# The end of a MoE router: rows of expert 0 by products of split parts, and a new order around them

## The chip, the cores and the metric

The kernel runs on one core of a Trainium2 chip. The metric is the device time of one execution in microseconds, given as the median of several runs. Beside these runs one execution was taken by the hardware profiler; all rows below come from it. TensorE multiplies, VectorE, ScalarE and GpSimd work on elements, SP issues DMAs; each works through a queue of its own in order.

## The reference

One decoder layer on 512 tokens of width 1024, in fp32: two token mixers, merged, then a mixture of experts, then an embedding gate. What matters here is the mixture of experts:

```
def hier_moe(h, w_rg, b_rg, w_re, b_re, w_e13, w_e2):
    t = h.reshape(b * s, dm)
    gl = (t @ w_rg) + b_rg                      # 4 groups
    pg = softmax(gl); gsel = top-1 of gl
    el = ((t @ w_re) + b_re)                    # 4 groups x 4 experts
    elg = el of the chosen group
    ev, ei = top_k(elg, 2)
    wts = pg[gsel] * softmax(ev)
    gate[token, expert] = wts
    a = t @ w_e13[e]                            # 1024 -> 2 x 256, 16 experts
    act = silu(g_) * u * gate
    y = sum over e of act @ w_e2[e]             # 256 -> 1024
```

Here h is the rms-normalized x after x = x + mixed @ w_out. The chip's products of full accuracy are made by splitting an fp32 value into a high part (fp32r) and a low part (the rest), and adding three products: high by high, high by low, low by high.

## The kernel before

**Weights.** All weights come as pieces of 128 x 1024 fp32 (512 KB) through one `Stream`. `_load` issues the DMA of a piece into a ring of raw buffers (WE, WE2, WR and WE3, 28 pieces for the experts' weights). `_split` makes the high part on ScalarE (L103) and the low part on VectorE (L106) into one of 4 slots of the pool WS; with `late_low` set, the low part is kept back as a function to be called later (L97 to L101). `ahead` and `get` run loads and splits in front of the use, `split_ahead` pieces, within `limit` and `raw_limit`. WE3's buffers are tiles of the pool `mx` (`freed`), which first hold mT, the split parts of the mixed output; so a load into them (tile name mT) waits until a block's products with mT are done.

**Router.** Tokens are worked on in four blocks b of 128. x2 holds x after the output product, half by half (c = 0, 1 of 512 columns). For each block the loop L1304 multiplies the second half (L1315, 24 products), adds it to x2 on VectorE (L1323), and calls `half`: GpSimd scales x2 into t (L1239), a DMA writes t to t_dram (L1240; ScalarE's queue for c = 0, SP's for c = 1), TensorE transposes x2 into tp (L1243), tp is copied to tT, and ScalarE squares for the norm (L1247). `logits` multiplies tT by the router's weights (L1255). `choose` (L1266 to L1285) is a chain of small VectorE instructions: norm, logits, best group, two best experts, hot, and then products on TensorE that count the tokens' places (pos_ps). `route` (L1288) makes oh0, the one-hot of a token's place within expert 0 (L1294), posk and two one-hots more, and multiplies these into slot_ps (L1300). choose and route of block b run inside block b + 1; those of the last block stand behind the loop.

**Router's end, L1327 to L1376.** `rows0` (L1332) gathers the rows of expert 0 on TensorE: acc0 += oh0 x t, in fp32, for four blocks and two halves. Two loads go to GpSimd's queue, three high parts of expert 0's weights to ScalarE (L97). After choose and route of the last block acc0 is copied to r0, one half by ScalarE and one by VectorE (L1362), gidx is made (L1363), the first low part lows[0] is made, r0 is transposed (L1369) and split into t0 (L1370, L1371), and rsl and the low parts that are left follow. cnt (L1359) is the largest count of an expert; all engines load it and branch over a block for overfull experts (L1413).

**Experts.** `gather(e)` fetches the rows of expert e from t_dram into tg by an indirect DMA from GpSimd (L1378), three experts ahead. The exponentials for the tokens' weights wts follow (L1384 to L1398); wts is first used behind the experts (L1651). `expert_in(e)` makes 24 products of 512 columns (L1510); `expert_T(e)` transposes tg and splits it into tgh and tgl (L1496 to L1498); for expert 0, `between` calls `expert_T(1)` ahead of the last of its four weight pieces (MID = 3). `expert_act` (silu, L1408), `expert_actT` and `expert_out` (L1535, 12 products; ye copied on ScalarE, L1539, and scattered to y_dram by GpSimd, L1540) follow. Behind the experts come `pp_start` and `pp_mm` (L1574), the loads of yy from y_dram, and the last stage.

**What sets the order.** The instructions are traced in the order of the text; a scheduler then orders each engine's queue by its own clock, an instruction that is ready early going ahead of an earlier traced one that is not. `issue_after(i)` (and `after`) ties what a block traces on i's engine behind i; `in_order()` ties all that it traces on each engine into the order of the text.

## Time and profile before

| | |
|---|---|
| time, median of 3 runs | 705.02 us (704.5 to 706.92) |
| the profiled execution | 707.7 us, of which the span from first to last instruction is 705.9 us |
| TensorE / VectorE / ScalarE / GpSimd busy | 684.4 (97%) / 561.5 (80%) / 434.5 (62%) / 139.1 us (20%) |
| granted TensorE clock | 0.998 of full speed |
| HBM | 108.41 MB read, 12.58 MB written, 171 GB/s over the span |

How to read it: busy times are those in which an engine ran an instruction; register, branch, semaphore and DMA-issuing instructions do not count. The router's loop runs from about 437 to 470 us, its end to 482, the sixteen experts to about 636, the last stage to 706. Matmuls overlap, so the distance between two starts is the cost of one, not its duration. A gap in a timeline stands in brackets with what ended it.

### The profile page before, as it was taken

To read this page: it belongs to the slowest core of one execution; us is meant where nothing else is said; L and a number is where in the kernel's file an instruction comes from. 1 tells how busy PE (TensorE), PEld (TensorE's weight loads), DVE (VectorE), ACT (ScalarE), POOL (GpSimd) and SP (SyncE) were. 2 spreads that over 40 slices of the span, in tenths; PEclk is the share of its full clock that TensorE was granted. 3 is DMA by queue.
4 is the path that set the end of the run, shared out by engine and by line. 5 is a ranking of instruction groups with operands and counts; after the bars stand their busy time and mean duration, and the time that the engine had idled before them with its cause. 6 is when DMAs were issued, how large, how long until landed. Compare 5 with 4: busy or idle time off the path is not lost.

```text
span 705.9 us, 11369 instructions
## 1 busy us (share of the span) xinstructions
PE 684.4 (97%) x3813; PEld 579.5 (82%) x3813; DVE 561.5 (80%) x1430; ACT 434.5 (62%) x848; POOL 139.1 (20%) x189
## 2 busy tenths in 40 slices
PE   8999989999999999999999999999999999999995
PEld 5889967789999998888888888876788888887784
DVE  5768988888768668878775763768999999986986
ACT  5547756576556765665453242236999999987642
POOL 5510033234334210000000002122222222110000
PEclk9999999999999999999999999999999999999999
DMA  8435631222212113232229348945999989507511
GB/s 290 110 96 151 168 100 37 84 61 61 61 31 59 32 40 82 61 91 64 86 63 354 121 124 284 372 150 189 384 386 374 370 299 364 234 30 265 194 61 61
DMA packets 81992, 113.72 MB, mean 161 GB/s; under 512 B 9417, under 2 KB 49945, under 8 KB 81930
## 3 DMA queue, kind: packets, MB, share of 16 engines
q1 hardware_dynamic: 72322, 97.14, 41.5%
q0 software_dynamic: 5648, 11.53, 4.5%
q10 hardware_dynamic: 3960, 4.29, 1.8%
q8 instruction: 31, 0.51, 0.3%
q14 instruction: 31, 0.25, 0.1%
HBM read 108.41 MB, written 12.58 MB: 171 GB/s over the span
## 4 chain that ended last, share of the span: by engine, by line
PE 74%; DVE 8%; DMA 7%; ACT 4%; issue 4%; POOL 3%; ACTq 0%; SPq 0%; POOLq 0%; DVEq 0%
PE S L1510 12%; PE mm L979 12%; PE mm L292 7%; PE mm L1682 6%; PE mm L1535 6%; PE mm L1151 6%; PE mm L802 3%; PE mm L1315 3%; PE tp L896 2%; DMA wr<-in_w_re 2%; PE S L875 2%; PE tp L1496 2%; DVE wlWS L106 2%; PE mm L912 1%; ACT whWS L103 1%
## 5 line engine op out<-in xcount | busy, mean ns | idle before, releaser
L106 DVE TENSOR_TENSOR wlWS<-rawWR,whWS 128x1024 fp32r<-128x1024 f32 (+3 forms) x75 | 85.9, 1153 | 25.5 <-ACT whWS L103 24.6
L103 ACT ACTIVATE whWS<-rawWR 128x1024 fp32r<-128x1024 f32 (+1 forms) x76 | 79.1, 1049 | 35.7 <-PE tp L1223 7.0
L106 DVE TENSOR_TENSOR wlWS<-rawWE,whWS 128x1024 fp32r<-128x1024 f32 x58 | 69.2, 1222 | 3.6 <-ACT whWS L103 2.3
L103 ACT ACTIVATE whWS<-rawWE 128x1024 fp32r<-128x1024 f32 x58 | 60.6, 1071 | 5.1 <-PE S L1510 4.1
L292 PE MATMUL mm<-wlWS,hTh 128*128 128x256 f32 (+1 forms) x184 | 54.2, 295 | 0.1
L292 PE MATMUL mm<-whWS,hTl 128*128 128x256 f32 (+1 forms) x184 | 54.2, 294 | 0.0
L292 PE MATMUL mm<-whWS,hTh 128*128 128x256 f32 (+1 forms) x184 | 53.9, 293 | 0.0
L979 PE MATMUL mm<-hTh,whWS 128*128 128x512 f32 x128 | 50.3, 393 | 0.0
L886 POOL TENSOR_SCALAR pr<-pr,sm 128x128 f32<-128x128 f32 (+3 forms) x64 | 34.7, 554 | 78.7 <-DVE sm L884 34.8
L979 PE MATMUL mm<-hTh,wlWS 128*128 128x512 f32 x128 | 50.0, 391 | 0.0
L979 PE MATMUL mm<-hTl,whWS 128*128 128x512 f32 x128 | 50.0, 391 | 0.0
L1510 PE MATMUL S<-whWS,tgh 128*128 128x512 f32 x120 | 48.6, 405 | 0.0
L1510 PE MATMUL S<-wlWS,tgh 128*128 128x512 f32 x120 | 47.8, 398 | 0.0
L1510 PE MATMUL S<-whWS,tgl 128*128 128x512 f32 x120 | 47.3, 395 | 0.0
L880 ACT ACTIVATE pr<-pr,sm 128x128 f32<-128x128 f32 (+3 forms) x64 | 35.4, 555 | 17.0 <-DVE sm L878 16.8
L899 ACT ACTIVATE ph<-tp 128x512 fp32r<-128x512 f32 (+1 forms) x48 | 25.1, 522 | 20.3 <-PE tp L896 19.8
L108 POOL TENSOR_TENSOR wlWS<-rawWR,whWS 128x384 fp32r<-128x384 f32 (+1 forms) x17 | 25.2, 1484 | 62.0 <-ACT whWS L103 57.1
L292 PEld LDWEIGHTS mm<-wlWS,hTh 128*128 128x128 f32 x184 | 34.9, 190 | 0.4 <-DVE wlWS L106 0.3
L292 PEld LDWEIGHTS mm<-whWS,hTl 128*128 128x128 f32 x184 | 34.9, 190 | 0.1
L292 PEld LDWEIGHTS mm<-whWS,hTh 128*128 128x128 f32 x184 | 34.9, 190 | 0.0
L1540 POOL DMA_INDIRECT y_dram<-ye,gidx x16 | 20.8, 1302 | 62.1 <-ACT aeh L1524 59.0
L876 DVE CUSTOM_DVE_ANT_0 pr<-S,strip 128x128 f32<-128x128 f32 (+3 forms) x64 | 29.3, 485 | 3.9 <-PE S L875 3.4
(492 smaller groups left out, 2076.8 us busy)
## 6 DMA issues: line engine op xcount, KB each, us to landing
rawWE<-in_w_e SPq DMA_DIRECT2D x59, 512.0 KB, 9.1
rawWR<-in_w_in SPq DMA_DIRECT2D x40, 512.0 KB, 3.9
mT<-in_w_e SPq DMA_DIRECT2D x22, 512.0 KB, 10.5
rawWR<-in_w_e SPq DMA_DIRECT2D x13, 512.0 KB, 10.1
rawWR<-in_w_out SPq DMA_DIRECT2D x8, 512.0 KB, 4.0
yy<-y_dram SPq DMA_DIRECT2D x8, 512.0 KB, 5.1
rawWR<-in_w_ck SPq DMA_DIRECT2D x4, 512.0 KB, 4.4
rawWR<-in_w_cv SPq DMA_DIRECT2D x4, 512.0 KB, 5.6
```

The source lines that it names most:

```text
L103: self.last_hi = self.nc.scalar.activation(h[:, :n], flat, AF.Copy)
L106: self.last = self.nc.vector.tensor_tensor(l[:, :c], flat[:, :c], h[:, :c].bitcast(F32), OP.subtract)
L108: self.nc.gpsimd.tensor_tensor(l[:, c:n], flat[:, c:], h[:, c:n].bitcast(F32), OP.subtract)
L292: T.matmul(dst[b], a[:, kk, b * P:(b + 1) * P], w[:, kk - k0, :n], start=(kk == 0 and i == 0 and b % share == 0), stop=(kk == NK - 1 and i ...
L876: V.tensor_tensor_reduce(pr[:, hh, :n], s_[:, :n], strip[:, 512 - q0:640], 0.125, -3.0e38, OP.add, OP.max, sm[:, 0, hh:hh + 1])
L880: A.activation(pr[:, hh, :n], pr[:, hh, :n], AF.Exp, bias=sm[:, 1, hh:hh + 1], accum_out=sm[:, 2, hh:hh + 1])
L886: G.tensor_scalar(pr[:, hh, :n], pr[:, hh, :n], sm[:, 3, hh:hh + 1], 1.0, op0=OP.mult, op1=OP.mult)
L979: T.matmul(ps, w[:, k], a[:, k], start=(k == 0 and i == 0), stop=(k == NK - 1 and i == 2))
L1151: T.matmul(ps, w[:, k, f * P:(f + 1) * P], a[:, k], start=(k == 0 and i == 0), stop=(k == 3 and i == 2))
L1510: T.matmul(ps, a[:, 2 * m + k], w[:, k], start=(m == 0 and k == 0 and i == 0), stop=(m == 3 and k == 1 and i == 2))
L1535: T.matmul(acc[c], a[:, k], w[:, 0, c * 512:(c + 1) * 512], start=(k == 0 and i == 0), stop=(k == 1 and i == 2))
L1682: T.matmul(acc, a[:, k], w[:, 0, lo:hi], start=(k == 0 and i == 0), stop=(k == NK - 1 and i == 2))
```

## The change

Rows of expert 0: each block's t is split into a high and a low part, thl[b], two more tiles of the pool mx. `t_high` (ScalarE) and `t_low` (VectorE, for the last quarter GpSimd) do this per half, t_low of the second half within `route`. rows0 multiplies oh0, now fp32r, by both parts: 16 products in place of 8 in fp32.

The end of the router stands in `in_order()`: the last block's transposes come ahead of rows0, rows0 of block 0 ahead of the last logits, blocks 1 and 2 behind them; rows0 of the last block comes right behind oh0 (`then`); both copies of acc0 go to ScalarE; gidx comes ahead of lows[0]; cnt and its products behind t0. A silu of one column is put on ScalarE behind the three high parts. The loads into WE3's buffers, two per block before, come all together behind this block, with the three of WE.

Expert 0's 24 products get an order of their own, its low parts later; expert 1's transposes are traced ahead of the last two, which are tied behind them. split_ahead is 2 during expert 0. The exponentials for wts move behind the last expert.

```diff
-        def rows0(b, c):
-            T.matmul(acc0[c], oh0[b], ts[b][:, c * 512:(c + 1) * 512], start=(b == 0), stop=(b == NB - 1),
-                     skip_group_check=True)
+        b, sl = NB - 1, slice(512, D)
+        def rows0(b, c):
+            for i in range(2):
+                T.matmul(acc0[c], oh0[b], thl[b][i][:, c * 512:(c + 1) * 512], start=(b == 0 and i == 0),
+                         stop=(b == NB - 1 and i == 1), skip_group_check=True)
...
+        def t_high(b, c):
+            if c == 0:
+                thl[b] = freed(F32R), freed(F32R)
+            sl = slice(c * 512, (c + 1) * 512)
+            A.activation(thl[b][0][:, sl], ts[b][:, sl], AF.Copy)
+        def t_low(b, c, eng=V):
+            sl = slice(c * 512, (c + 1) * 512)
+            return eng.tensor_tensor(thl[b][1][:, sl], ts[b][:, sl], thl[b][0][:, sl].bitcast(F32), OP.subtract)
...
@@ half @@
+            if c and b < NB - 1:
+                t_high(b, 0)
+            if c:
+                t_low(b, 0)
+                t_high(b, 1)
+                if b == NB - 1:
+                    t_low(b, 1, G)
...
@@ route @@
+            if b < NB - 1:
+                t_low(b, 1)
...
@@ the loop over blocks @@
-            if b + 1 < NB:
-                st.raw_limit += 2
-                st.ahead(st.n_split - 1 - st.split_ahead)
...
+        with in_order():
+            logits(b, 0)
+            t_high(b, 0)
+            V.scalar_tensor_tensor(x2[:, b, sl], ps, 0.5, x2[:, b, sl], op0=OP.mult, op1=OP.add)
+            half(b, 1)
+            rows0(0, 0)
+            rows0(0, 1)
+            logits(b, 1)
+            for bb in range(1, b):
+                for c in range(2):
+                    rows0(bb, c)
...
+            sil = op_.tile([P, 1], F32, name="sil")
+            A.activation(sil, ss2[:, 0, 0:1], AF.Silu)
...
+            oo, placed = choose(b)
+            route(b, oo, lambda: [rows0(b, c) for c in range(2)])
+            r0 = op_.tile([P, D], F32, name="t", bufs=1)
+            for c in range(2):
+                A.activation(r0[:, c * 512:(c + 1) * 512], acc0[c], AF.Copy)
+            V.tensor_scalar(gidx, slot_ps[:, 0:32].rearrange("p (a e) -> p a e", a=2), BIG, None, op0=OP.add)
             lows[0]()
...
+        st.raw_limit += N_WE3 + N_WS - 1
+        st.ahead(st.n_split - 1 - st.split_ahead)
...
@@ expert_in, for expert 0 @@
+            mm(0, th_, w[0][0])
+            mm(1, th_, w[1][0])
+            mm(0, th_, w[0][1])
+            mm(0, tl_, w[0][0])
+            mm(1, tl_, w[1][0])
+            w.append(st.get(("e1", e, 2)))
+            mm(2, th_, w[2][0])
+            mm(2, tl_, w[2][0])
+            mm(1, th_, w[1][1])
+            w.append(st.get(("e1", e, 3)))
+            mm(3, th_, w[3][0])
+            mm(3, tl_, w[3][0])
+            mm(2, th_, w[2][1])
+            turned, hi = between()
+            with after(turned):
+                mm(3, th_, w[3][1])
+            return ps, hi
...
     copied = expert_out(15, *aa)
+    ge = rt.tile([P, NB, 4], F32, name="ge")
+    with tc.issue_after(aet[1].ins):
+        V.tensor_tensor(ge, lg[:, :, 0:4], g8[:, :, 0:1].to_broadcast([P, NB, 4]), OP.subtract)
+    A.activation(ge, ge, AF.Exp)
...
```

## Rows read from the trace of the kernel before

**Rows 1.** Page, part 1, TensorE: busy us (share) and instructions.

```profile
PE 684.4 (97%) x3813; PEld 579.5 (82%) x3813; DVE 561.5 (80%) x1430; ACT 434.5 (62%) x848; POOL 139.1 (20%) x189
```

**Rows 2.** Windows by stage, engines' busy us (instructions), clock, DMA, GB/s.

```profile
core 0: us, PE busy (x) PEld busy (x) DVE busy (x) ACT busy (x) POOL busy (x), PEclk, DMA share, GB/s
...
445.08:454.28 9.20, 9.20 (x61) 7.78 (x59) 6.36 (x30) 2.44 (x7) 2.17 (x2) 1.00 1.05 405
...
470.12:481.92 11.80, 11.31 (x59) 6.64 (x58) 7.77 (x33) 5.35 (x8) 4.36 (x5) 1.00 0.48 151
481.92:490.13 8.21, 6.99 (x34) 5.23 (x33) 7.12 (x14) 5.71 (x9) 1.99 (x3) 1.00 0.56 160
490.13:497.25 7.12, 7.10 (x35) 5.21 (x34) 6.71 (x11) 7.09 (x10) 0.03 (x1) 1.00 1.03 398
...
516.42:525.89 9.47, 9.47 (x48) 7.77 (x47) 9.08 (x11) 8.72 (x13) 2.13 (x2) 1.00 1.04 395
```

**Rows 3.** Chain of waits, whole span: start, us, what; one steady expert.

```profile
525.02 0.87 PE tp L1496 x8
...
528.89 5.58 PE S L1510 x24
```

**Rows 4.** Chain of waits, router's end: the two transfers before expert 1.

```profile
472.01 4.71 DMA t_dram<-tg
...
479.55 5.60 DMA tg<-t_dram,gidx
```

**Rows 5.** Timeline, TensorE: start, us, line, operation, tiles [idle before, releaser].

```profile
478.70 1.95 PE L1332 MATMUL mm<-tg,oh 128*128 128x512 f32 x4
...
485.29 0.63 PE L1496 MATMUL tp<-ident,tg 128*128 128x128 f32 x4 [1.22 <-DMA tg<-t_dram,gidx]
...
490.13 0.40 PE L1510 MATMUL S<-whWS,tgh 128*128 128x512 f32 x1
```

**Rows 6.** Timeline, VectorE, in the loop (two rows) and behind it.

```profile
454.12 0.69 DVE L1245 COPY tT<-tp 128x512 f32<-128x512 f32 x1 [1.04 <-PE tp L1243]
...
459.67 0.16 DVE L1292 SCALAR_TENSOR_TENSOR p<-S,hot 128x1 f32<-128x1 f32 x1 [0.68 <-PE S L1284]
...
481.89 0.69 DVE L1371 TENSOR_TENSOR wlWS<-tp,whWS 128x512 fp32r<-128x512 f32 x1 [0.43 <-ACT whWS L1370]
```

**Rows 7.** Timeline, VectorE, router's end and the start of the experts.

```profile
474.40 0.24 DVE L1269 SCALAR_TENSOR_TENSOR lg<-o,tokc,brt 128x24 f32<-128x24 f32 x1 [0.63 <-PE o L1255]
...
477.94 1.22 DVE L100 TENSOR_TENSOR wlWS<-rawWE,whWS 128x1024 fp32r<-128x1024 f32 x1
479.07 0.18 DVE L1363 TENSOR_SCALAR gidx<-S 128x32 int32<-128x32 f32 x1
...
483.45 2.59 DVE L100 TENSOR_TENSOR wlWS<-rawWE,whWS 128x1024 fp32r<-128x1024 f32 x2
...
488.09 0.17 DVE L1389 TENSOR_REDUCE pgs<-ge 128x4 f32<-128x16 f32 x1 [0.76 <-ACT ge L1387]
```

**Rows 8.** Timeline, SP: first of the pairs of moved loads.

```profile
446.73 0.81 SPq L77 DMA_DIRECT2D mT<-in_w_e  x2
```

**Rows 9.** Tile view of tg, all gathers: issue to landing.

```profile
DMA to landing us min/median/max: 3.2/7.2/10.2
```

**Rows 10.** Timeline, ScalarE: around the second table load.

```profile
490.43 1.05 ACT L103 ACTIVATE whWS<-rawWE 128x1024 fp32r<-128x1024 f32 x1
491.50 1.28 ACT L1408 ACT_TABLE_LOAD   x1
492.80 0.48 ACT L1408 ACTIVATE sg<-S,rsl 128x256 f32<-128x256 f32 x1
```

**Rows 11.** Timelines of ScalarE, GpSimd and TensorE at the end of the experts.

```profile
635.35 1.29 ACT L1539 ACTIVATE ye<-mm 128x512 f32<-128x512 f32 x2 [0.18 <-PE mm L1535]
...
636.91 0.97 POOL L1540 DMA_INDIRECT y_dram<-ye,gidx  x1 [3.15 <-ACT ye L1539]
...
647.75 0.63 PE L1655 MATMUL tp<-ident,x 128*128 128x128 f32 x4 [0.51 <-DVE x L1651]
```

More of the change, by code (lines that the diff above doesn't have):

```diff
@@ L32 @@
 N_WARM = 10
-MID, M_POS = 3, 3
+M_POS = 3
 FILL_A = 12.0, 10.3, 6.8, 7.2
@@ L1318, in tile_hybrid @@
                 route(b - 1, oo)
[L1319 to L1321 removed]
+            if b == NB - 1:
+                break
             logits(b, 0)
             V.scalar_tensor_tensor(x2[:, b, 512:], ps, 0.5, x2[:, b, 512:], op0=OP.mult, op1=OP.add)
[L1324 to L1326 removed]
+            half(b + 1, 0)
+            half(b, 1)
             logits(b, 1)
@@ L1343, in tile_hybrid @@
-        st.limit += N_WS - 1
-        st.raw_limit += N_WS - 1
-        st.late_low = []
-        with tc.issue_after(sq.ins), tc.issue_after(tTc.ins):
-            st.ahead(st.n_split + 2 * (N_WS - 4) + 1)
-        lows, st.late_low = st.late_low, None
-        t0 = [t.rearrange("p (k t) -> p k t", k=NK) for t in split_from("WS")()]
-        oo, placed = choose(NB - 1)
-        made = route(NB - 1, oo)
-        with after(placed):
-            for c in range(2):
-                for b in (NB - 2, NB - 1):
-                    rows0(b, c)
```

102 lines of the change are left out of this document (49 added, 53 removed).

## The prediction

> **What bounds the kernel now.** The page comes first: TensorE is busy for 97% of the 705.9 us span [rows 1]. That says only that its idle time is short, so the next view is by stage [rows 2]. An expert in the steady phase takes 9.47 us, with TensorE busy for all of it, VectorE for 9.08 and ScalarE for 8.72; a product of 512 columns costs 0.2325 us there (24 in 5.58) and eight transposes 0.87 [rows 3]. Nothing can be won in that phase but work that TensorE no longer does. The stretch ahead of it is different. From the last router block's logits to the first product of expert 0 (470.12 to 481.92) TensorE is busy 11.31 of 11.80 us, from there to expert 1's first product 6.99 of 8.21, and from there to the first product of expert 0's second layer at 497.25 7.10 of 7.12. The second of these holds idle time, the first holds work that may be too dear.
>
> The chain of waits through that stretch [rows 4] runs over no product of the router: write of the last half block to t_dram (4.71 us, landing at 476.72), gather of expert 1's rows (5.60 us from 479.55, landing at 485.15), and then TensorE without a break. The 2.8 us between the two transfers are the wait for gidx, which VectorE makes at 479.07 [rows 7]. The gather's landing sets TensorE: the transposes of expert 1 stand in its queue behind only 7 of expert 0's 24 products, and TensorE waits 1.22 us for them at 485.29 [rows 5]. So 17 products come behind the transposes, and the start of expert 1 follows as landing + 0.14 + 0.87 + 17 x 0.2325 = 490.11; the first product of expert 1 is at 490.13 [rows 5]. This formula carries the forecast.
>
> **The change part by part.** *Rows of expert 0.* Eight fp32 products go, each two passes in the trace; four passes take 1.95 us [rows 5], so up to 7.8 us of TensorE. Sixteen on split parts come, 16 x 0.2325 = 3.7 by rows 3, and only four of them (0.93) still stand behind the last one-hot. None of this is a gain by itself: what comes behind has to be ready. The high parts cost ScalarE two copies a block, the low parts VectorE two subtractions of 0.69 each (one on GpSimd in the last block); the row is a subtraction of the same size [rows 6].
>
> *Inside the loop.* VectorE idles 0.68 us in each block while it waits for the position product [rows 6]; the low part of the second half is put right there. The first half's low part meets the gap of 1.04 ahead of the copy of tT. What sticks out may hold up the products that wait for hot: up to 1.4 us for each of three blocks if the cover is gone, a few hundredths if it holds. I take +0.2 in all, the nearer row being the gap.
>
> *Transposes of the last half first.* The logit of the last block waited 0.63 us for TensorE at 474.40, VectorE having been ready at 473.77 [rows 7]. With rows0 behind the transposes and not between them, VectorE's own chain sets it: 0.5 us earlier, and all of choose and route with it.
>
> *Low parts later.* gidx stands behind lows[0] on VectorE now (1.22 us from 477.94); it goes ahead. It then follows the slot products: last one-hot 0.5 earlier, four short products 0.93, slot products 0.5, so about 478.3 in place of 479.07. The gather is issued 0.8 us earlier, at 478.75.
>
> *The loads that move.* Eight 512 KB loads (mT) are issued today in pairs, beside blocks 0 to 2 by SP [rows 8], the last pair by GpSimd. They move behind the router and wait for thl, which now lives in their buffers; by the products that free these, SP issues them from about 472.5 to 478.4. In a stretch with loads queued DMA moves 405 GB/s [rows 2], 1.3 us a load, so they keep DMA busy until about 483 and share it with the gather. SP's queue has the t_dram write in front of them, GpSimd's loses two issues ahead of its last multiplication. Bounds for the gather's landing time: 5.6 us as today, or 7.2, the median of the 15, most of which run beside weight loads [rows 9]; the slowest took 10.2. I take 7.2, as loads will stand in the queues: landing 485.95. The Trainium skill ("DMA: Bandwidth & Descriptors", Issuing engines are not separate DMA queues) says that DMAs of all issuing engines run on the same 16 DMA engines and interleave, which speaks against this part of the change; the trace's 7.2 beside 5.6 agrees, and by the rule the lower bound would not be reached.
>
> *Order of expert 0.* 22 products are traced ahead of expert 1's transposes and two behind. Are the 22 done by then? The second acc0 was done at 480.65 and its copy to r0 waited for VectorE; now it is done near 477.8. Copies, transposes and th of the first half follow by about 479.4, and 22 x 0.2325 = 5.1 brings TensorE to 484.5. The last low part of three ends at 486.04 today [rows 7] and about 2.6 earlier in the new order, 483.4, in time for the 21st product. The branch on cnt, which each engine takes, lies in the 1.5 us that are left until 486. So expert 1 starts at 485.95 + 0.14 + 0.87 + 2 x 0.2325 = 487.4, 2.7 us earlier.
>
> *Exponentials and tables.* Two table loads of 1.28 us leave ScalarE's queue between 486 and 493, and VectorE's wait of 0.76 for the exponential goes [rows 7, 10]. Expert 1's stretch of 7.12 us holds 24 x 0.2325 + 0.87 + 0.14 = 6.6 of work, so 0.5 can be had there; VectorE has about 9 us of low parts and the rest to do from 483.4 until the second layer's first weights, to 492.4, ahead of TensorE at 494.0. I take 0.5 of gain: 3.2 us at the second layer. The load for silu moves to ScalarE's queue between the weights' high parts and the copies of r0: from about 475.6 to 477.1, and the copies wait for rows0 until 477.4. Here the row shows one activation ending at 491.48, the load from 491.50 and the next activation at 492.80 [rows 10]: 1.3 us for the switch.
> The Trainium skill ("ScalarE: Activation LUTs", What ACT_TABLE_LOAD costs) gives 1283 ns and another 1380 ns of drain. The load agrees, the drain is not in this trace. By the rule, r0's copies would come 1.1 us later, within the 1.5 in hand, and the end would pay up to 1.4 more: an estimate of 703.9 by that page.
>
> *The end.* Behind the last expert ScalarE now has a table load and two small exponentials, 1.28 + 0.4. It lands beside the copies of ye at 635.35 and 636.04, whose end releases the scatter at 636.91, and from there by way of the yy loads the x at 647.75, where TensorE has waited 0.51 [rows 11]. If all of it falls ahead of ye the end moves by 1.7; if ye keeps its place, it delays the products of pp, which have that 0.51 in hand. I take +0.5, between 0 and 1.7, since ye is traced ahead of the exponentials.
>
> Sum: -3.2 + 0.2 + 0.5 = -2.5. The profiled execution (707.7 with its 705.9 span) would become 705.2; the median of 705.02 becomes 702.5.
>
> **The rivals.** (1) *The order does not hold.* Only the last two products are tied behind the transposes; the scheduler may still put these earlier, as it did with 18 traced ahead and 7 issued. With nine behind them expert 1 starts at 485.95 + 0.14 + 0.87 + 2.1 = 489.05, gain 1.1 + 0.4 there, and the total is 704.2. For it: today's order. Against it: low parts are traced late enough that no product ahead should lack one. (2) *Gather as today*, 5.6 us: expert 1 at 485.8, then VectorE's 492.4 and the second layer bound it: 4.85 earlier, 0.7 paid back, 700.9. (3) *The end pays in full*: -3.2 + 0.2 + 1.7, 703.7. (4) *Gather as the slowest*, 10.2: expert 1 at 490.4; -0.1 + 0.7, 705.6. (5) *Slower: the write behind the loads.* If SP issues the last half block's write to t_dram behind the moved loads, and not at 472.0, it waits for the buffers that rows0 of the last block frees at 477.8, and its data for eight loads, until about 485; then 5.6 to 7.2 of gather, expert 1 at 492 to 493.7, 2 to 3.6 later than now, 0.5 of it won back in its stretch and 0.7 paid elsewhere: 707.2 to 708.8, 708.0 in the middle. It decides as soon as that write is issued later than about 476. Against it: it is traced first, and its input is there at 472.0.
>
> **How the numbers follow.** Forecast 0.52 (own range 701.0 to 703.7), (1) 0.13, (2) 0.14, (3) 0.08, (4) 0.05, (5) 0.08. A measurement of this kernel tells 0.3%, 2.1 us, from no change, so faster is below 702.9: two thirds of the forecast's case, all of (2), a little of (1) and (3), 0.52. Slower, over 707.1, is (5), 0.08; 0.40 lies between. The range leaves out the lower edge of (2), (5) and part of (4): 700.6 to 705.6.
>
> **What would show it.** Right are gidx near 478.3, a gather issued before 479 and landing after 485.5, two products of expert 0 behind the eight transposes, first product of expert 1 near 487.4, second layer near 494.0, no table load between 480 and 500 and one near the last scatter. Wrong would be a t_dram write after 476, many products behind the transposes, new idle time of TensorE inside the loop's blocks, or, at the end, more than today's 0.51 us of TensorE's wait for x.

## The result, and the profile after

The changed kernel takes 711.96 us (median of 6 runs, 709.35 to 713.16) against 705.75 for the kernel before in the same runs: a ratio of 1.0079, 95% interval 1.0065 to 1.0093. It is 6.2 us slower; the forecast was 2.5 us faster. Two of the executions behind the table of experiments, one of fp32_rows_loads_in_loop (842.39 us) and one of all_mended (750.10), ran at a mean granted clock of 0.75 and 0.85 and are left out of all medians and ratios. The profiled execution has a span of 710.6 us, TensorE's busy time is a little less than in [rows 1], and its idle time is longer:

```profile
PE 683.5 (96%) x3813; PEld 581.3 (82%) x3813; DVE 568.9 (80%) x1436; ACT 440.2 (62%) x858; POOL 139.7 (20%) x188
```

The profiled executions start the router up to 3 us apart (434.8 to 437.9 us over the kernels of this document), so all that follows is counted from the first product of the second half (the loop L1315, L1336 in the changed kernel): 437.40 us before, 436.58 after. The stretches between the same instructions, in us:

| stretch, ending with | before | forecast | after |
|---|---|---|---|
| the last half's x (VectorE) | 32.54 | 32.74 | 35.56 |
| gidx | 9.13 | 8.36 | 9.86 |
| first transpose of expert 1 | 6.22 | 7.79 | 10.15 |
| first product of expert 1 | 4.84 | 1.33 | 1.38 |
| second layer of expert 0 | 7.12 | 6.62 | 7.39 |
| ye of expert 15 | 138.10 | 138.10 | 138.10 |
| first transposes of the last stage | 12.40 | 12.90 | 13.58 |
| end of the span | 58.15 | 58.15 | 58.03 |
| sum | 268.50 | 265.99 | 274.05 |

One row came out as forecast (two products behind the transposes, 1.38), the experts' steady phase is untouched, and five rows are each 0.7 to 2.8 us worse than forecast: 8.1 us in all. The windows cut at these instructions, of the kernel before and then of the changed one (columns as in [rows 2]), and as the third line of the second fence one extra window for the clock:

```profile
437.40:469.94 32.54, 31.94 (x188) 26.39 (x186) 21.05 (x90) 6.86 (x16) 8.15 (x7) 1.00 0.75 274
469.94:479.07 9.13, 8.85 (x45) 5.42 (x44) 6.96 (x29) 4.65 (x7) 2.44 (x3) 1.00 0.47 145
479.07:490.13 11.06, 9.63 (x48) 6.63 (x47) 8.11 (x18) 6.41 (x11) 4.05 (x4) 1.00 0.54 160
...
635.35:647.75 12.40, 11.89 (x52) 9.14 (x51) 7.49 (x9) 9.01 (x14) 1.57 (x2) 1.00 0.64 204
```

```profile
436.58:472.14 35.56, 33.65 (x196) 27.36 (x194) 26.45 (x97) 10.66 (x23) 8.35 (x7) 1.00 0.45 164
472.14:482.00 9.86, 7.40 (x42) 5.89 (x42) 7.21 (x30) 7.86 (x12) 2.97 (x2) 0.91 0.67 213
480.16:483.58 3.42, 3.42 (x17) 3.14 (x16) 1.63 (x5) 1.79 (x3) 1.11 (x1) 0.50 1.02 394
482.00:493.53 11.53, 8.42 (x44) 6.81 (x44) 8.63 (x11) 4.81 (x7) 4.16 (x4) 0.93 1.03 391
493.53:500.92 7.39, 7.18 (x36) 5.38 (x35) 7.28 (x9) 6.66 (x10) 0.95 (x1) 1.00 0.43 129
...
639.02:652.60 13.58, 12.30 (x52) 9.12 (x51) 8.81 (x15) 10.43 (x17) 1.56 (x2) 1.00 0.65 228
```

The third line of the second fence is what no part of the prediction mentions: from 480.16 to 483.58 the granted clock is 0.50, the lower of its two levels (1.2 in place of 2.4 GHz), while TensorE has work all the time. TensorE's timeline shows what stood ahead of that and what follows (brackets: idle time before, and what ended it):

```profile
478.87 0.17 PE L1301 MATMUL S<-hot,trs 128*128 128x16 bf16 x1 [1.50 <-DVE hot L1299]
479.61 1.63 PE L1353 MATMUL mm<-mT,oh 128*128 128x512 f32 x4 [0.58 <-DVE oh L1313]
...
481.76 1.94 PE L1386 MATMUL tp<-ident,t 128*128 128x128 f32 x8
...
485.28 1.16 PE L1514 MATMUL S<-whWS 128*128 128x512 f32 x4 [1.50 <-DVE cnt L1392]
...
492.15 1.06 PE L1501 MATMUL tp<-ident,tg 128*128 128x128 f32 x8 [1.61 <-DVEq L1418]
...
493.53 0.50 PE L1541 MATMUL S<-whWS,tgh 128*128 128x512 f32 x1
```

In the kernel before the last hot costs TensorE 0.28 us, and expert 0 follows r0's transposes at once:

```profile
476.50 0.17 PE L1284 MATMUL S<-hot,trs 128*128 128x16 bf16 x1 [0.28 <-DVE hot L1282]
...
481.92 0.50 PE L1510 MATMUL S<-whWS 128*128 128x512 f32 x1
```

In the changed kernel TensorE waited 1.50 us for the last hot and 0.58 for the last one-hot, then the clock fell; it waited 1.50 more for cnt ahead of expert 0, and 1.61 ahead of expert 1's transposes, not for the gather, which had landed at 490.47, but for VectorE's branch. VectorE's timeline of that stretch answers to [rows 7]:

```profile
476.76 0.24 DVE L1286 SCALAR_TENSOR_TENSOR lg<-o,tokc,brt 128x24 f32<-128x24 f32 x1
...
482.00 0.19 DVE L1381 TENSOR_SCALAR gidx<-S 128x32 int32<-128x32 f32 x1 [1.60 <-PE S L1321]
482.10 1.22 DVE L100 TENSOR_TENSOR wlWS<-rawWE,whWS 128x1024 fp32r<-128x1024 f32 x1
...
485.05 0.17 DVE L1392 TENSOR_REDUCE cnt<-S 128x1 int32<-128x16 f32 x1
...
488.50 3.50 DVE L106 TENSOR_TENSOR wlWS<-rawWE,whWS 128x1024 fp32r<-128x1024 f32 x3 [1.02 <-ACT whWS L103]
```

Counted from the loop's first product gidx comes 3.75 us later than before (45.42 against 41.67), cnt stands behind both low parts of t0, and three low parts of the weights (3.50 us) stand ahead of the branch that ends at 492.0. GpSimd's issue of the gather took 1.09 us before and 1.89 now; the tile view gives its time from issue to landing, 5.6 before ([rows 4]) and 8.0 now. First the kernel before, then the changed one:

```profile
479.55 1.09 POOL L1378 DMA_INDIRECT tg<-t_dram,gidx  x1 [7.01 <-DVE gidx L1363]
```

```profile
482.47 1.89 POOL L1399 DMA_INDIRECT tg<-t_dram,gidx  x1 [5.85 <-DMA mT<-in_w_e]
...
DMA to landing us min/median/max: 8.0/8.0/8.0
```

### The profile page after: what moved, and what is told of

The parts are those of the page before. It is cut to its first block, busy times and chain, and to the rows that moved or that the text cites. A ratio compares the mean times of both kernels' runs of the same rounds, so it can differ in the third digit from the quotient of the medians.

```text
span 710.6 us, 11387 instructions
## 1 busy us (share of the span) xinstructions
PE 683.5 (96%) x3813; PEld 581.3 (82%) x3813; DVE 568.9 (80%) x1436; ACT 440.2 (62%) x858; POOL 139.7 (20%) x188
```

## The experiments

All distances below are in us from the loop's first product, read in the profiled execution as above; "half" is the time around the router's end in which the granted clock was 0.50 (the last 3 to 6 us of every trace are at 0.50 too, and logits_behind had another 3.41 us at 107.62). Distances and "half" are of one execution each: kernels whose loop is the same differ by up to 0.5 us in x (32.03 and 32.54; 35.26 to 35.68), and other executions of a kernel can have another clock (four of cnt_early: 0.997, 0.997, 0.996, and 0.991 with 711.67 us). Times are medians; ratios are against the kernel before in the same session (its medians were 705.50 to 706.09), with 95% intervals. Where two versions' intervals overlap, their times do not tell them apart.

| kernel | x | gidx | expert 0 | transposes of 1 | expert 1 | end stage | half | time | ratio |
|---|---|---|---|---|---|---|---|---|---|
| before | 32.54 | 41.67 | 44.52 | 47.89 | 52.74 | 12.40 | none | 705.75 | 1 |
| changed | 35.56 | 45.42 | 48.70 | 55.57 | 56.95 | 13.58 | 3.41 | 711.96 | 1.0079 (1.0065, 1.0093) |
| fp32_rows | 32.34 | 43.15 | 45.90 | 52.98 | 54.40 | 13.60 | 3.41 | 709.42 | 1.0055 (1.0034, 1.0075) |
| fp32_rows_loads_in_loop | 32.47 | 43.28 | 46.03 | 53.09 | 54.52 | 13.60 | 3.41 | 708.53 | 1.0033 (1.0020, 1.0045) |
| no_branch | 35.26 | 44.35 | 47.10 | 53.39 | 54.77 | 13.59 | none | 709.42 | 1.0048 (1.0032, 1.0063) |
| cnt_early | 35.45 | 44.54 | 45.77 | 53.78 | 55.15 | 13.61 | none | 710.06 | 1.0068 (1.0043, 1.0094) |
| exps_front | 35.68 | 44.75 | 47.90 | 57.87 | 60.51 | 12.43 | 10.24 | 713.68 | 1.0108 (1.0087, 1.0128) |
| before_exps_behind | 32.03 | 41.17 | 44.01 | 47.07 | 51.92 | 13.61 | none | 706.96 | 1.0018 (1.0006, 1.0030) |
| gather_first | 35.30 | 44.56 | 45.78 | 53.08 | 54.45 | 13.61 | none | 710.15 | 1.0080 (1.0053, 1.0106) |
| gather_first_no_branch | 35.35 | 45.82 | 47.40 | 52.51 | 53.85 | 13.60 | 3.41 | 708.05 | 1.0020 (1.0006, 1.0033) |
| high_behind | 34.36 | 43.57 | 45.26 | 52.74 | 54.11 | 13.58 | 3.41 | 709.44 | 1.0051 (1.0035, 1.0068) |
| logits_behind | 34.16 | 44.39 | 46.03 | 53.35 | 54.72 | 13.58 | 3.41 | 709.12 | 1.0034 (1.0018, 1.0051) |
| lows_on_gpsimd | 33.47 | 42.63 | 44.32 | 51.95 | 53.32 | 13.58 | 3.41 | 708.32 | 1.0028 (1.0018, 1.0038) |
| all_mended | 32.95 | 42.75 | 44.44 | 50.33 | 51.67 | 12.40 | 3.41 | 705.96 | 0.9996 (0.9981, 1.0011) |
| fp32_cnt_early | 32.73 | 43.53 | 44.76 | 51.58 | 53.04 | 13.60 | none | 706.20 | 1.0005 (0.9990, 1.0020) |
| fp32_cnt_early_low_first | 32.46 | 43.26 | 44.49 | 50.03 | 51.46 | 13.59 | none | 705.92 | 1.0004 (0.9995, 1.0014) |
| fp32_cnt_early_tanh | 32.44 | 43.24 | 44.46 | 50.22 | 51.65 | 12.94 | none | 704.47 | 0.9984 (0.9970, 0.9997) |
| fp32_cnt_early_tanh_low_first | 32.54 | 43.34 | 44.56 | 50.10 | 51.52 | 12.45 | none | 704.72 | 0.9991 (0.9980, 1.0002) |

Theory ahead of the runs: the split parts cost the loop, the gather shares DMA with loads, VectorE's late counts and branch hold TensorE, and the exponentials cost the end. Rival: the new order or the clock alone does it.

### Split parts undone, and the loads with them

```diff
-            for i in range(2):
-                T.matmul(acc0[c], oh0[b], thl[b][i][:, c * 512:(c + 1) * 512], ...)
+            T.matmul(acc0[c], oh0[b], ts[b][:, c * 512:(c + 1) * 512], ...)
...
-                t_low(b, 0)
-                t_high(b, 1)
```

> The changed kernel with expert 0's rows in fp32 as before (no split parts of t, so two ScalarE copies and two subtractions a block less; everything else of the change stays, the moved loads too). Theory (the split parts hold up the loop and VectorE's chain): the last half's x, at 472.14 us in the changed kernel and 469.94 before, is back between 469.9 and 470.9; gidx, 482.00 in the changed kernel, is near 480; the gather still flies about 8 us; the time falls from 712.0 to 709.5-710.5. Rival (the loop's delay comes from the new order and the moved loads): x stays at 472 +- 0.3 and the time at 712 +- 0.7.

The last half's x is back at 32.34, so the loop's 3.0 us come with the split parts and none with the new order. The moved loads came back into the loop too, as shown next; that they are not the cause shows in all_mended below, which keeps them out of the loop and has x at 32.95. The median is 709.42 and not 711.96, though the intervals of the ratios overlap. From x to gidx the split parts are the cheaper ones: 9.09 at full clock (no_branch, cnt_early) against 10.81 here, since the last block's fp32 products, 1.98 us from 476.83, now stand between the one-hot and the slot products. One expectation fell: the gather flies 5.7 us here, not 8. SP's timeline says why, first of the changed kernel, then of fp32_rows: without the split parts in WE3's buffers the scheduler puts the moved loads back beside the blocks, whatever the text's order, and the last one is issued 9 us ahead of the gather.

```profile
474.61 0.32 SPq L1251 DMA_DIRECT2D t_dram<-tg  x1
475.03 6.67 SPq L77 DMA_DIRECT2D mT<-in_w_e  x8
```

```profile
445.05 5.95 SPq L77 DMA_DIRECT2D mT<-in_w_e  x3
...
453.35 6.38 SPq L77 DMA_DIRECT2D mT<-in_w_e  x2
...
462.10 6.43 SPq L77 DMA_DIRECT2D mT<-in_w_e  x2
...
470.93 1.10 SPq L77 DMA_DIRECT2D mT<-in_w_e  x1
```

> The kernel fp32_rows with the eight loads put back beside the blocks, two each, the last two on GpSimd's queue. Theory (the moved loads share DMA with the gather): its flight, 5.60 us before and 8.00 in the changed kernel, falls to 5.5-6.3, expert 1's first product comes 0 to 2.4 us earlier than in fp32_rows (the wait for the branch may take the place), time 707.5-709. Rival (the flight is set by something else, such as the write of t or GpSimd): flight 7.5-8.5 and the time that of fp32_rows within 0.5.

```diff
+            st.raw_limit += 2
+            st.ahead(st.n_split - 1 - st.split_ahead)
             logits(b, 0)
```

So this kernel is nearly the last one again: flight 5.7, all distances within 0.15, 0.9 us less with intervals that overlap. It tells nothing of its two theories apart; gather_first below does.

Both still wait ahead of expert 0, and both have the clock at half from the end of that wait on:

```profile
481.99 2.04 PE L1503 MATMUL S<-whWS 128*128 128x512 f32 x4 [1.74 <-DVE cnt L1381]
```

```profile
481.90:485.31 3.41, 3.33 (x8) 2.68 (x9) 2.29 (x3) 0.00 (x0) 3.02 (x2) 0.50 0.90 312
```

At full clock the 22 products take 5.1 us (22 x 0.2325), here 7.07 pass from the first of them to the transposes (481.99 to 489.06), with no idle time: in this execution the clock costs nearly 2 us of what the undoing gives.

### The waits for cnt and for the branch

```diff
-    most = nc.values_load(cnt[0:1, 0:1], min_val=64, max_val=S)
-    with tc.If(most > P):
-        ...
```

> The changed kernel without the block for overfull experts and without its branch on cnt (that part is left out). Theory (TensorE waits for the branch twice: 1.50 us ahead of expert 0's first product and 1.61 us ahead of expert 1's transposes, the second on the path): expert 0 starts near 483.8, the transposes of expert 1 follow the gather's landing (490.5) by 0.2 us and come 1.5 us earlier, time 710.2-710.7. Rival (the wait for the branch covers another wait that ends at the same time, such as the one for VectorE's low parts): the transposes stay at 491.8-492.2, time 711.5-712.3.

Half of it holds. The transposes of expert 1 follow the gather's landing by 0.13 and come 2.2 us earlier, of which 0.6 is the gather's own landing (53.26 against 53.89): this execution had the clock at full, so that gidx came earlier. The time is below the 710.2 expected. But expert 0 still waits, 1.70 us, and for the same instruction; a branch was never in it:

```profile
484.15 1.17 PE L1445 MATMUL S<-whWS 128*128 128x512 f32 x4 [1.70 <-DVE cnt L1392]
...
490.44 1.06 PE L1432 MATMUL tp<-ident,tg 128*128 128x128 f32 x8 [1.02 <-DMA tg<-t_dram,gidx]
```

What expert 0's first product needs is the accumulator: pos_ps, slot_ps and the experts' sums are three tiles named S with two buffers, and the counts hold one until VectorE has reduced them to cnt, which the change put behind t0's two low parts.

```diff
+            for bb in range(NB):
+                T.matmul(pos_ps[:, 64:80], trs[:, 1], hot[:, bb], ...)
+            V.tensor_reduce(cnt, pos_ps[:, 64:80], AX.X, OP.max)
+            V.tensor_copy(rsl, slot_ps[:, 32:48])
             lows[0]()
```

> The changed kernel with the counts' products and the reduction to cnt put right behind gidx, ahead of lows[0]. Theory (expert 0's first product waits for the accumulator named S that the counts hold until VectorE's reduction, which the change put behind both low parts of t0; VectorE's branch, behind three more low parts, then holds expert 1's transposes): expert 0's first product, 485.28 us in the changed kernel, comes at 483.6-484.2; the transposes of expert 1, 492.15, follow the gather's landing (490.2-490.6) by less than 0.3; time 709.5-710.7. Rival (the granted clock at half from 480.17 to 483.58 alone is what costs): it stays at half for as long, the transposes stay at 491.8 or later, time 711.5-712.5.

```profile
481.48 1.20 PE L1514 MATMUL S<-whWS 128*128 128x512 f32 x4 [0.25 <-ACT whWS L1391]
...
489.49 1.06 PE L1501 MATMUL tp<-ident,tg 128*128 128x128 f32 x8 [2.72 <-DMA tg<-t_dram,gidx]
```

The wait of 1.50 goes to 0.25 and expert 0 starts 2.9 earlier; no wait for the branch shows any more. The clock stays at full in this execution. Yet expert 1's transposes still come 53.78 behind the loop's first product, since TensorE now waits 2.72 us for a gather that flies 8.6: one wait has taken the place of the other. The median is 710.06 and not 711.96, with intervals of the ratios that overlap. The rival, that the clock alone costs, falls: with the clock at full the span from the loop's first product is 272.36, still 3.9 longer than the 268.50 before.

### The gather and the loads in front of it

```diff
     for e in range(1, N_TG + 1):
         gather(e)
+    st.queue = nc.gpsimd
+    st.raw_limit += N_WE3 + N_WS - 1
+    st.ahead(st.n_split - 1 - st.split_ahead)
+    st.queue = nc.sync
```

> cnt_early (split parts, granted clock full) with the eleven loads issued by GpSimd behind the three gathers in place of by SP ahead of them. Theory (the loads that wait for the split parts' buffers lie in the DMA queues beside the gather, which flies 8.62 us in cnt_early and 5.7 in fp32_rows, whose loads had landed by 475.3): flight 5.3-6.3; TensorE's wait of 2.72 us for the gather shrinks to 0-0.7, expert 1 starts 2.0-2.7 earlier, time 707.3-708.4. Rival (the gather is slow because GpSimd takes 2.05 us to issue it beside VectorE's low part, 1.09 before): flight stays above 7.5, time that of cnt_early within 0.7.

```profile
474.70 1.30 POOL L77 DMA_DIRECT2D mT<-in_w_e  x2
479.85 1.99 POOL L1397 DMA_INDIRECT tg<-t_dram,gidx  x1 [3.85 <-DVE rsl L1385]
482.14 1.94 POOL L1397 DMA_INDIRECT tg<-t_dram,gidx  x1 [0.30 <-issue]
...
486.32 3.35 POOL L77 DMA_DIRECT2D mT<-in_w_e  x5
```

Three of the eleven loads stay ahead (one at 472.80, two at 474.70), the others now follow the gathers. TensorE's wait shrinks only from 2.72 to 2.01 us and ends with the branch again, which stands behind three low parts on VectorE; the trace of this kernel has no landing for the gather. The time stays at cnt_early's, as the rival said and not the theory (707.3 to 708.4); its four executions run from 708.49 to 713.37. So the same kernel was run without the branch:

> gather_first without the block for overfull experts and its branch (that part is left out). In gather_first the gather's data had moved by 484.5 us, but TensorE's transposes waited 2.01 us more, until VectorE's branch behind three low parts. Theory (with the loads behind the gather the branch is what ends last): without it the transposes of expert 1 follow the 22 products, 15.8-16.2 us behind the last half's x (17.8 in gather_first, 18.3 in cnt_early), no wait for the gather above 0.4; time 707.7-708.8. Rival (the gather still flies about 8 us and would end at the same time as the branch): a wait for the gather of 1.5 us or more, time 709.5 or more.

```profile
483.59 1.99 POOL L1397 DMA_INDIRECT tg<-t_dram,gidx  x1 [5.07 <-DVE rsl L1385]
...
DMA to landing us min/median/max: 5.0/5.0/5.0
```

The tile view gives 5.0 us from issue to landing (483.59 to 488.62), and TensorE has no wait for the gather any more, although GpSimd's issue took 1.99. That settles the flight: 8.0 to 8.6 us with the loads issued in front (the six such kernels whose trace has the landing; no_branch, 8.4, has no branch either), 5.0 and 5.2 with eight of them behind (this one and all_mended), the same rows on the same queue. The time is as expected, the transposes come 17.2 behind x and not 16, because the clock was at half from 480.34 to 483.75: from hot to gidx it takes 3.79, against 2.58 in gather_first.

### What in the split parts delays the loop

```diff
-                t_high(b, 1)
+                with after(copied):
+                    t_high(b, 1)
```

> cnt_early with each block's high part of the second half tied behind the copy of tT on ScalarE. Theory (in the loop ScalarE's high parts stand ahead of the copies that the logits wait for: TensorE's waits of 0.32 and 0.44 us for tT): both waits go, the last half's x, 35.45 us behind the loop's first product in cnt_early and 32.54 before, comes at 34.3-34.9; the rest of the 2.9 stays with VectorE (one-hots late by 0.69) and the logits' place; time 0.6-1.1 less than cnt_early. Rival (ScalarE alone holds up the loop): x at 33.0 or earlier, time 2 or more less. Second rival (VectorE alone): x within 0.3 of 35.45.

```diff
+            with after(lastmm):
-            logits(b, 0)
+                logits(b, 0)
```

> high_behind with the last block's first logits (8 short fp32 passes, 0.89 us) tied behind its 24th product. Theory (what stands ahead of the last products on TensorE delays x by its own length): the last half's x goes from 34.36 us behind the loop's first product to 33.4-33.6; time 0.5-1 less than high_behind. Rival (VectorE, not TensorE, then sets x and the logit): x at 34.0 or later or the logit no earlier, time the same within 0.4.

```diff
-                t_low(b, 0)
+                t_low(b, 0, G)
...
-                t_low(b, 1)
+                t_low(b, 1, G)
```

> high_behind with the low parts of blocks 0 to 2 on GpSimd in place of VectorE (the scheduler then also puts the last block's first logits behind the products). Theory (what is left of the loop's delay, 34.36 against 32.54 before, is 0.9 of logits and VectorE's low parts, 0.69 us of late one-hots): x at 32.5-33.0; time 1.2-2 less than high_behind. Rival (GpSimd's subtractions of 1.3 us hold up its own products of x and so t, the high parts and the gather): x at 33.4 or later, time no less than logits_behind.

The first puts ScalarE's second high part behind the copy of tT in all blocks: x goes from 35.45 to 34.36, as expected, and TensorE's two waits for tT go. In the changed kernel this order stood so (ScalarE; TensorE's logits waited 0.33 and 0.45 us for these copies in two blocks):

```profile
445.56 0.63 ACT L1238 ACTIVATE mT<-t 128x512 fp32r<-128x512 f32 x1 [0.96 <-POOL t L1250]
446.10 0.58 ACT L1260 ACTIVATE tT<-tp 128x512 f32<-128x512 f32 x1
```

Tying the last logits behind the products brings only 0.2 of the 0.9 expected: TensorE then waits 0.56 us for hot in its place, its rival. The low parts of blocks 0 to 2 on GpSimd bring 0.7 more, 33.47: just past the rival's 33.4 and not the theory's 33.0, while the time, 708.32, is no worse than that of logits_behind, as the rival would have had it. So of the 2.9 us in cnt_early about 1.1 go with ScalarE's order, 0.7 with VectorE's low parts, and 0.2 with the logits' place, which is no more than one execution differs from another; 0.9 is not told apart by these runs. VectorE and GpSimd also hold each other up: one of the six low parts in the loop, which I priced at 0.69, takes 1.40 beside GpSimd's product of 1.28; what that costs x is not told apart.

```profile
454.31 1.40 DVE L1242 TENSOR_TENSOR mT<-tg,mT 128x512 fp32r<-128x512 f32 x1
```

### The exponentials

```diff
+    ge = rt.tile([P, NB, 4], F32, name="ge")
+    with tc.issue_after(lo0.ins):
+        V.tensor_tensor(ge, lg[:, :, 0:4], g8[:, :, 0:1].to_broadcast([P, NB, 4]), OP.subtract)
+    A.activation(ge, ge, AF.Exp)
...
     def silu_gate(out_, ps, gain):
...
     copied = expert_out(15, *aa)
-    ge = rt.tile([P, NB, 4], F32, name="ge")
...
```

> The changed kernel with the exponentials for the tokens' weights back in front of the experts. Theory (they cost the end 1.2 us, from expert 15's ye, 3.67 us late, to the final stage's first transposes, 4.85 us late): that difference goes to 0 +- 0.2; two table loads of 1.28 us return near expert 1 and cost there 0 to 0.7; time 710.8-711.6. Rival (the end is late for another reason, such as expert 0's order or the loads): the difference stays at 1.2 and the time is 712.0-712.7.

The other kernel has this move alone, the other way, on the kernel before:

> The kernel before with one part of the change alone: the exponentials behind the experts. Theory: the start gains 0.3-0.7 (second layer of expert 0 at 496.5-497.0 and not 497.25), the end loses 1.2, so 0.5-0.9 slower than before: 706.2-706.6. Rival (the two table loads ahead of expert 1 cost the start as much as the exponentials cost the end): the second layer comes 1.2 or more earlier and the time is that of before within 0.3.

The end is as expected in both: 12.43 with the exponentials in front, 13.58 to 13.61 with them behind, in all thirteen kernels that have them there. On the kernel before this part alone costs 1.2 us at the end, gains 0.5 from x to the second layer (27.31 to 26.81), and is slower: 1.0018 (706.96, a little above the 706.2 to 706.6 expected). In front of the new order they cost far more than the 0 to 0.7 expected, 3.6 us at expert 1 (713.68, not 710.8 to 711.6): the table load at 489.12 stands ahead of VectorE's small steps, these ahead of its branch, and TensorE waits 2.92 us for that, with the clock at half for 10.24 us in all, 6.83 more than in the changed kernel; the 3.6 us hold both.

```profile
489.12 1.28 ACT L1414 ACT_TABLE_LOAD   x1
```

ScalarE's end in the changed kernel shows where the 1.2 come from. Before, in front of the first ye of [rows 11]:

```profile
634.10 1.07 ACT L103 ACTIVATE whWS<-rawWE 128x1024 fp32r<-128x1024 f32 x1
```

After, the first ye is not late, but the load has the place that the weights' next high part had ahead of it; now that part comes at 641.04, 3.3 us later against ye, and the second ye is 0.4 late. The copies of pp's products and the scaled weights follow 0.9 to 2.2 us late, and VectorE's adds to x, at 650.92, stand in its queue behind the low parts of those weights, where TensorE waits 0.83 us for them and not the 0.51 of [rows 11]. That it is the table load and not the two small exponentials shows in all_mended, which has tanh in the same place, no table load, and an end stage of 12.40.

```profile
637.42 1.28 ACT L1629 ACT_TABLE_LOAD   x1
638.71 0.22 ACT L1629 ACTIVATE ge<-ge 128x16 f32<-128x16 f32 x1
639.02 0.60 ACT L1570 ACTIVATE ye<-mm 128x512 f32<-128x512 f32 x1
639.52 0.20 ACT L1636 ACTIVATE e<-e 128x4 f32<-128x4 f32 x1
639.61 0.59 ACT L1593 ACTIVATE mT<-tp 128x512 fp32r<-128x512 f32 x1
640.09 0.60 ACT L1570 ACTIVATE ye<-mm 128x512 f32<-128x512 f32 x1
...
641.04 1.08 ACT L103 ACTIVATE whWS<-rawWE 128x1024 fp32r<-128x1024 f32 x1
```

### Versions put together

The first is the edits of fp32_rows and cnt_early together:

> fp32_rows (rows of expert 0 in fp32) with the counts put ahead in the same way. Theory: TensorE's idle 1.74 us ahead of expert 0 goes, the first product comes at 480.2-480.6, the 22 products are done by 485.6, the gather lands near 485.4 and sets expert 1 again: first product at 486.8-487.2 (490.13 before), second layer of expert 0 at 493.7-494.4 (497.25 before); the end costs 1.2; time 702.8-704.2. Rival (the half clock of fp32_rows, 481.90 to 485.31, comes whatever the idle time): the 22 products take 6.8 us and not 5.1, expert 1 at 488.5-488.9, time 705-706.

```diff
     ps, hi1 = expert_in(0, lambda: expert_T(1))
     st.split_ahead = 3
+    ge = rt.tile([P, NB, 4], F32, name="ge")
...
+    A.activation(ge, ge, AF.Tanh, scale=0.5)
+    V.tensor_scalar(ge, ge, -1.0, 1.0, op0=OP.mult, op1=OP.add)
+    V.reciprocal(ge, ge)
+    pgs = rt.tile([P, NB], F32, name="pgs")
+    V.tensor_reduce(pgs, ge, AX.X, OP.add)
+    V.tensor_scalar(pgs, pgs, 2.0, -4.0, op0=OP.mult, op1=OP.add)
...
     copied = expert_out(15, *aa)
-    ge = rt.tile([P, NB, 4], F32, name="ge")
...
-    A.activation(ge, ge, AF.Exp)
...
```

> fp32_cnt_early with the tokens' weights behind expert 0's first products in place of behind the experts, and with tanh, which is in silu's table, in place of exp: exp(x) = (1 + tanh(x/2)) / (1 - tanh(x/2)). Theory (the end pays 1.2 us for the table load and two exponentials on ScalarE): no table load behind 480, the distance from expert 15's ye to the last stage's first transposes goes from 13.60 back to 12.40, time 1.0-1.4 less than fp32_cnt_early. Rival (VectorE's ten small instructions, some 1.7 us, now hold up expert 1's low parts): the second layer of expert 0 comes 1 to 1.7 later and the time is that of fp32_cnt_early within 0.5.

```diff
+            lows[0]()
             V.tensor_scalar(gidx, slot_ps[:, 0:32].rearrange("p (a e) -> p a e", a=2), BIG, None, op0=OP.add)
...
-            lows[0]()
```

> fp32_cnt_early with the first low part back ahead of gidx. Theory (beside VectorE's subtraction GpSimd needs 2.05 us to issue the gather, alone 1.09, so that gidx ahead of lows[0] gains nothing): the issue takes 1.0-1.2 us, gidx stays within 0.2 of its place behind the one-hots since VectorE idles there, the flight falls from 7.44 to 5.3-6.0, expert 1 starts 0.4-0.95 earlier, time 705.2-706. Rival (gidx is delayed by the low part, 1.22 us, as before): gidx 0.5-1.2 later, expert 1 no earlier, time 706-707.2.

> fp32_cnt_early_tanh with the first low part ahead of gidx. Theory (there TensorE's 22 products and not the gather set expert 1's transposes, no idle time ahead of them): no gain, the time that of fp32_cnt_early_tanh, 704.5, within 0.7. Rival (the gather still sets it in most executions): 703.3-703.8.

With fp32 rows and the counts early expert 0 starts at 44.76 and the clock stays up, as expected; but the gather took 7.4 us and TensorE waited 0.95 for it; the time is 706.2 and not 702.8 to 704.2. The wait explains 0.95 us of that, and the rest is not told apart. With the low part back ahead of gidx GpSimd issues in 1.17 us, gidx is not late, expert 1 comes 1.6 earlier, more than the 0.4 to 0.95 expected, and TensorE's 22 products set it; the median falls by 0.3 only, inside the intervals. How much of a slow flight is the slow issue stays open: with an issue of 1.8 to 2.05 the flights were 5.7, 5.7, 5.9 and 7.4 in the kernels with fp32 rows, and 5.0 and 5.2 at 1.99 with split parts.

With tanh no table load is left behind 480, the end stage is 12.94 and 12.45, and the time 704.47 and 704.72, within the 0.7 of each other that was expected: about 1 us less than the kernel before (0.9984, 0.9970 to 0.9997 for the first; the second's interval reaches 1.0002). The pair with the low part first differs in the tanh and its place alone: 705.92 to 704.72, the end from 13.59 to 12.45. This version, the new order without the split parts and without the move of the exponentials, has the only interval below 1 among the sixteen tried, and by 0.0003: that it beats the kernel before is likely, not shown.

The last kernel keeps the split parts and has the edits of cnt_early, gather_first_no_branch, high_behind, logits_behind and lows_on_gpsimd and the tanh together:

> The changed kernel with split parts kept and all that was found to cost put right: counts early, high parts behind the copies, low parts on GpSimd, logits behind, loads behind the gathers, tanh in place of the exponentials behind the experts; the branch and the block for overfull experts are left out. Theory (the four costs found make up the difference, and the split parts then save their 3.5 us on TensorE): expert 1's first product at 49.8-50.8 us behind the loop's first product (52.74 before, 56.95 in the changed kernel), the end's 13.58 back to 12.4-12.9, time 703.0-704.5. Rival (something else that was not found keeps a microsecond or more): time 705 or more.

With everything mended that was found, split parts kept and the branch left out, expert 1 comes at 51.67, 1.1 earlier than before, the end stage is back at 12.40, and the profiled span from the loop's first product is 1.4 shorter; the median is 705.96, the ratio 0.9996, not to be told from the kernel before. So the mends together make up the loss, though two things in this version, the missing branch and the tanh, were not tried on the kernel before (its TensorE shows no wait for the branch). The gain that the forecast put on top does not appear: TensorE waits 1.94 us for the last hot, and the clock falls to half at 478.92. The expected 703.0 to 704.5 was wrong, and its rival (705 or more) holds by the time.

What stands behind the last hot shows in these traces. A small step of VectorE ahead of the last logit, tokc with two columns, takes 0.23 us in all four blocks before and in all kernels with fp32 rows. In the last block it takes 0.52 in the changed kernel, beside GpSimd's low part (475.32, 1.30 us), and 1.62 in all_mended, where GpSimd issues a load from 472.44 and makes a low part from 473.11 to 474.43. First the kernel before, then all_mended:

```profile
473.53 0.23 DVE L227 TENSOR_SCALAR tokc<-rs_m 128x2 f32<-128x2 f32 x1
```

```profile
472.84 1.62 DVE L227 TENSOR_SCALAR tokc<-rs_m 128x2 f32<-128x2 f32 x1
```

From x to the last logit it is 5.35 us in all_mended and 4.26 in fp32_rows. By these rows the last block's low part on GpSimd, and the loads issued there, delay the very chain that the change was to shorten; no run moves them alone.

## Why the prediction was wrong, point by point

The forecast's first step that failed is the one inside the loop (+0.2), and the largest: 2.8 of the 8.1 us between forecast and trace. The second is the formula for the start of expert 1, in which only the gather could hold the transposes: gidx comes 1.5 us later than forecast, the transposes another 2.4.

- **Loop, +0.2; measured +3.02.** The step asked only what of VectorE's two subtractions sticks out of VectorE's gaps. It did not ask what is queued behind ScalarE's copies (tT, and so the logits: 1.1 us), nor what GpSimd and VectorE do to each other (0.69 became 1.40 in one of six). The upper bound, 1.4 for each of three blocks, would have covered it; I put it aside for the nearer row, where the low part meets a gap. fp32_rows shows that all of it comes with the split parts; 0.9 of it has no cause shown.
- **gidx, -0.8; measured +0.73 from x.** Transposes first gave the logit 0.2 (x to logit 4.46 before, 4.25 in fp32_rows), not 0.5; beside the split parts it is 4.62, of which 0.3 is tokc beside GpSimd. From hot to gidx the forecast -0.3 holds at full clock (2.80 before, 2.57 in cnt_early), and the half clock makes it 3.36 in the profiled execution.
- **Gather, 7.2; measured 8.0.** The mechanism was right, the size too small by 0.8: the loads were issued until 481.7 and landed until 489.8, not until 483. With most of them behind the gather it is 5.0 and 5.2. That the loads are late only because the split parts sit in their buffers was said, but not priced as a cost of the split parts.
- **Expert 0's start and the branch, priced at nothing; measured 1.50 and 1.61.** "cnt and its products behind t0" was listed in the change and had no step. The branch had one sentence, that it lies in the 1.5 us left until 486; it ends at 492.0, 1.5 behind the gather's landing. Expert 0 was to start at about 479.4, 42 us behind the loop's first product, and starts at 48.70. The accumulator that the counts hold, and the branch behind whatever the scheduler puts ahead of it, were the waits that took the place of the removed ones.
- **Two products behind the transposes, -3.5; measured -3.46.** Right, and rival (1) with it out; but it gains only when what releases the transposes does not come later.
- **Stretch of expert 1, -0.5; measured +0.27.** VectorE's low parts were to be 2.6 us earlier; they are later, since t0 is.
- **End, +0.5; measured +1.18.** The size: the table load stands ahead of ye and of pp's weights, nearer to the upper bound of 1.7 than to the 0.5 taken. The drain of 1.38 us that the Trainium skill gives ("ScalarE: Activation LUTs", What ACT_TABLE_LOAD costs) does not show here either: load at 637.42, 1.28 us, next activation at 638.71.
- **The clock, no step.** Every term was taken at the clock of the kernel before, and no step asked whether the clock would stay up. In the six runs of the changed kernel the mean granted clock is 0.992 to 0.996 and goes with the time (0.996: 709.35 and 710.14; 0.992: 713.16). That mean also holds the kernel's last microseconds at 0.50, so it does not say where the clock fell. As far as it goes the clock is the smaller part of the loss: the two runs at 0.996 are still 3.6 and 4.4 us slower than the kernel before. Why it fell stays open.
- **Rivals.** None of the five came; the slower one did not either: the write to t_dram went out at 474.61, ahead of the loads. The chance of slower, 0.08, rested on that single mechanism. Two of the four signs of being wrong that the prediction named did come: new idle time inside the loop's blocks (0.33, 0.45 and 0.69 us) and, at the end, 0.83 us of waiting for x in place of 0.51.

## What to carry to other kernels

Price a step that is added beside a busy engine by what is queued behind it on its own engine, copies on ScalarE included, and at the time it takes beside the neighbour that is busy then. When a load is moved or its buffer is given to something else, look where its issue goes against the one latency-bound transfer on the path. And when a wait is taken off the path, list the next two waits for the same engine with their times (accumulator, branch): here products, gather and branch ended within 1.6 us of one another (490.4, 490.47, 492.0), so each repair alone gave little.

## What the runs showed of the hardware

- **The clock fell at the router's end in nine of eighteen traces.** The granted clock fell to 0.50 for 3.41 us (6.83 in exps_front) behind waits of TensorE of 1.2 to 1.9 us for the last hot and 0.57 for the one-hot (seven kernels with split parts), or of 0.58 and 1.74 (fp32_rows and fp32_rows_loads_in_loop). Waits of 1.5 to 1.7 and 0.57 left it at full in no_branch, cnt_early and gather_first. In the six kernels whose wait for the last hot was at most 0.28 us and any other at most 1.22 it stayed at full, the kernel before among them. So the waits alone do not decide: the changed kernel (1.50 and 0.58, fell) and cnt_early (1.51 and 0.57, stayed) have the same ones. What does stays open. The Trainium skill ("TensorE: Matmul & The Clock Gate", What's actually happening) says that the clock has two states, 1.2 and 2.4 GHz, and follows how busy TensorE has been; the two levels agree with all eighteen traces, which hold 0.50 and 1.00 and nothing else.
- **GpSimd and VectorE hold each other up.** GpSimd's issue of an expert's gather at the router's end takes 1.0 to 1.2 us alone or where a low part is nearly over, and 1.8 to 2.05 where a low part of 1.22 began up to 0.4 us ahead of it (482.10 to 483.3 in the changed kernel; the issue ends 1.05 behind it). The Trainium skill ("SBUF — State Buffer", SBUF: two separate sides) says that a VectorE instruction can lock GpSimd out of a port that they share, so that GpSimd cannot write the descriptors of a DMA that it issues; its example is a copy, here it is a subtraction, and the rows agree. They show the other direction too: a subtraction of 0.69 that takes 1.40, and a step of 0.23 that takes 1.62.
- **A branch stands in an engine's queue.** In the changed kernel VectorE's branch ends at 492.0, with the last of the three low parts ahead of it. TensorE's wait for it, 1.61 us there, 2.01 in gather_first and 2.92 in exps_front, is gone where the branch is left out.
